# A hybrid mLSTM layer step: stabiliser rows by selector products, masks by selects, inter-chunk term scaled apart

## The chip, the cores and the metric

The kernel runs on one core of a Trainium2 chip. The metric is the device time of one execution in microseconds (us). The kernel before takes 1770.03 us, the median of three runs (1768.39 to 1771.12).

Engine names in what follows: PE is the tensor engine (PEld its weight loads), DVE the vector engine, ACT the scalar engine, POOL the GpSimd engine, SP the engine that issues most DMAs.

## What is computed

One layer of a flow-matching backbone for 128 context tokens and 256 latent tokens (384 in all, width 2048). Two parallel mixers follow one input projection: a bidirectional chunkwise mLSTM with 8 heads of 128, and a pooling mixer. Their outputs go through one output projection; a squared-ReLU MLP with hidden width 8192 follows. Scale, shift and gate of each token group come from a modulation product, `silu(c) @ ada_w`, over 6 x 2048 columns. The part that the change is about is the scan, for every head, direction and chunk of 128 tokens:

```python
b = jnp.cumsum(lfc, axis=-1)
dmat = jnp.where(mask, b[..., :, None] - b[..., None, :] + lic[..., None, :], -jnp.inf)
m_inter = b + m[..., None]
m_t = jnp.maximum(m_inter, jnp.max(dmat, axis=-1))
s = jnp.einsum('bhtd,bhsd->bhts', qc, kc) * jnp.exp(dmat - m_t[..., None])
g = jnp.exp(m_inter - m_t)
num = g[..., None] * jnp.einsum('bhtd,bhde->bhte', qc, C) + jnp.einsum('bhts,bhse->bhte', s, vc)
den = g * jnp.einsum('bhtd,bhd->bht', qc, n) + jnp.sum(s, axis=-1)
h = num / jnp.maximum(jnp.abs(den), jnp.exp(-m_t))[..., None]
```

In words: `m_t` is a stabiliser per token t; the score of tokens s and t is weighted by exp(a_s - m_t) where s lies on the right side of t (the mask), and what earlier chunks contribute (the inter-chunk term, through the state C) is weighted by g_t.

## The kernel before

Large products are made in three fp32r matmuls (high x high, high x low, low x high parts). `load_w` (L114) issues the load of a 512 KB weight block on SP, has ACT copy its high part (L126) and DVE subtract for its low part (L127); three raw blocks and four high/low blocks are in flight. `gemm_T` (L158) makes 256 columns of a product in four weight blocks, 24 matmuls of 384 columns each; a block with its matmuls is called a chunk below. Behind every chunk each `Feed` (L142) emits some steps of side work, at its own rate. In the order in time:

- Transposes of x, then u, v and the gate inputs, with the first two parts of the modulation beside them.
- `qk(0)`: q and k of heads 0 and 1, fed by `gates` (L434: cumulative sums, running maxima m, g; it ends by storing the rows m and g to `m_dram` and `g_dram`, L486 and L488), `pooling`, and modulation work.
- `qk(1)` to `qk(3)` and the o product: each `attention(hp)` (L521) handles the two heads of the pair before, in eight steps, one per chunk. Its first step loads by POOL's queue the rows m and g of the pair, broadcast to 128 partitions (`mbc`, `gbc`, L528 and L529, one buffer each), and the cached state C. Its second step does scores and transposed keys on PE; `decays` (L545) subtracts the rows from a mask of 0 and -1e30 on DVE (L548), takes the exponential on ACT (L551, 12 for a pair) and multiplies with the scores (L553). `update` (L568) makes new states. POOL multiplies q by the broadcast g (L629), so that `outputs` (L582) can accumulate the inter-chunk product in the same PSUM bank as the product with v (L589, L592). DVE, ACT and POOL then normalise (L594 to L601; the power of -0.5 is on POOL, L188), and the seventh step after transposes the heads on PE (L640).
- The modulation parts 2, 4 and 3 run beside all this: part 2 by `ada_mat` on PE (L203, feed `ada1`), parts 4 and 3 by `ada_vec` on DVE (L244, feed `ada2`): for every 512 columns 8 loads of 512 KB, each followed at once, in the same step, by its four accumulations on DVE (L255, L257). The raw blocks of both share four buffers.
- o, the output projection (w_out), then the MLP, which takes the last 1100 us.

Each engine runs its instructions in the order in which they were scheduled when the program was built; an instruction that waits holds everything behind it on its engine.

Of the kernel before, what the change touches and what calls it, by code (L numbers as in the profile page):

```python
# [13 lines left out]
P = 128  # L14
# [24 lines left out]
def hymba_kernel(  # L39
# [21 lines left out]
    # ---------------------------------------------------------------- constants and small inputs  # L61
# [26 lines left out]
    for d in range(2):  # L88
        nc.gpsimd.dma_start(mprev[32 * d:32 * d + 8, 1:2], state_m[0, 0, d, :].unsqueeze(1))
# [6 lines left out]
    # silu(c); for every contraction tile in a row of zeros, so that a window of 32 columns puts it in any pair of rows  # L96
# [9 lines left out]
    # per-channel parameters as columns: prmT [128, 80 | 96]  # L106
# [35 lines left out]
    class Feed:  # L142
        """Side work, emitted in steps between the tiles of a large product."""
# [14 lines left out]
    def gemm_T(w, cols, xs, n, evac, feeds=(), korder=(0, 1, 2, 3), name="g", hold=None):  # L158
        """Transposed products: for every 256-column group, out[128 channels, n] in two tiles; groups share the k loop."""
# [39 lines left out]
    # ---------------------------------------------------------------- adaLN  # L199
# [3 lines left out]
    def ada_mat(parts, tags=("ada",)):  # L203
        """parts: up to four (i, first channel tile), nk channel tiles each, on the tensor engine.
        Row 32 g + 2 b + (0: ctx, 1: latent) of ps holds part b's sum over the contraction tiles j = g (mod 4)."""
# [16 lines left out]
        sb = wp.tile([P, 256], F32, tag="adasb", name=f"ada_sb_{parts[0][0]}_{parts[0][1]}", bufs=2)  # L222
# [8 lines left out]
    def ada_finish(i, k0, nk, ps):  # L231
        """ps [128, nk, 2]: matrix product columns -> mod[i], with what the channel's norm weight adds to it"""
# [11 lines left out]
    def ada_vec(i, q):  # L244
        """512 channels, on the vector engine; the tensor engine adds up the partitions"""
        acc = wp.tile([P, 2, 512], F32, tag="adaacc", name=f"ada_acc_{i}_{q}", bufs=1)
        c0 = i * D + q * 512
        for t in range(8):
            raw = wp.tile([P, 2, 512], F32, tag="ada", name=f"ada_raw_{i}_{q}_{t}", bufs=N_ADA)
            nc.sync.dma_start(raw, aw[:, 2 * t:2 * t + 2, c0:c0 + 512])  # L250
            for a in range(2):
                for g in range(2):
                    cj = sg[:, g, 2 * t + a:2 * t + a + 1]
# [69 lines left out]
    # ---------------------------------------------------------------- h, and u, v, gates (token-major), k outermost  # L323
# [76 lines left out]
    # ---------------------------------------------------------------- pooling mixer  # L400
# [27 lines left out]
    m_dram = dram.tile([2, 3, 8, P], F32, name="m_dram")  # L428
    g_dram = dram.tile([2, 2, 8, P], F32, name="g_dram")
    acol = vp.tile([P, 3, 2, 8], F32, name="acol")  # L430
    ecol = vp.tile([P, 3, 8, 2], F32, name="ecol")
    nT = vp.tile([P, 16], F32, name="nT")

    def gates():  # L434
# [24 lines left out]
        aS, bS, mS, gS = [slot(n)[0:40, 0:NTOK].rearrange("p (s t) -> p s t", t=P) for n in ("aS", "bS", "mS", "gS")]  # L459
        for t in (aS, bS, mS):  # L460
            nc.gpsimd.memset(t, 0.0)
        for d in range(2):
            r = slice(32 * d, 32 * d + 8)
            nc.vector.tensor_copy(aS[r], ps_a[r, 0:NTOK].rearrange("p (s t) -> p s t", t=P))
            nc.scalar.activation(bS[r], ps_b[r, 0:NTOK].rearrange("p (s t) -> p s t", t=P), AF.Copy)
        mnew = vp.tile([40, 1], F32, name="mnew")
        for s in range(3):
            for d in range(2):
                r = slice(32 * d, 32 * d + 8)
                src = aS[r, s, :] if d == 0 else aS[r, s, ::-1]  # L470
                dst = mS[r, s, :] if d == 0 else mS[r, s, ::-1]
                nc.vector.tensor_tensor_scan(dst, src, src, mprev[r, s:s + 1], op0=ALU.max, op1=ALU.max)
                if s < 2:
                    out = mnew[r] if s == 0 else mprev[r, 2:3]
                    nc.vector.tensor_tensor(out, bS[r, s, last[d]:last[d] + 1], mS[r, s, last[d]:last[d] + 1], op=ALU.add)
                    if s == 0:
                        nc.gpsimd.dma_start(new_m[0, 0, d, :].unsqueeze(1), mnew[r])
        for s in (1, 2):
            nc.scalar.activation(gS[:, s, :], mS[:, s, :], AF.Exp, scale=-1.0, bias=mprev[:, s:s + 1])
        nc.vector.tensor_tensor(bS, bS, mS, op=ALU.add)  # L480
        nc.scalar.activation(bS, bS, AF.Exp, scale=-1.0)
        for d in range(2):
# [7 lines left out]
        for src, which in ((aS, 0), (bS, 1)):  # L490
# [557 lines left out]
```

## Time and profile before

| what | value |
|---|---|
| three timed runs | 1768.39, 1770.03, 1771.12 us |
| profiled execution: span from first to last instruction | 1766.4 us |
| its own time | not listed apart; the timed runs lie 2.0 to 4.7 us above this span |
| PE busy | 1719.2 us, 97% |
| DVE busy | 1067.4 us, 60% |
| ACT busy | 627.3 us, 36% |
| POOL busy | 129.7 us, 7% |
| granted PE clock, mean | 0.994 |
| chain that ended last | PE 86%, DMA 5%, issue 3%, DVE 2%, POOL 2%, ACT 1% |

How to read it: busy shares are means over stages with different limits. Matmuls are pipelined, so a busy PE is read from the distance between the starts of its instructions and not from the length of one. The granted clock is given in shares of full speed. Idle time of an engine is listed with what ended it.

### The profile page before, as it was taken

What the parts mean: (1) busy time and instruction counts of PE and PEld (TensorE: products, weight loads), DVE (VectorE), ACT (ScalarE), POOL (GpSimd) and SP (SyncE); (2) the same over time, 40 slices, a digit from 0 to 9 for tenths busy, and PEclk for the clock granted to TensorE, in tenths of its full rate; (3) what the DMA queues carried; (4) which work ended last, traced back from release to release, by engine and by line L of the source; (5) the groups of instructions that cost most, each with busy time, mean ns of one, the idle gap of its engine ahead of it and who ended that gap; (6) DMA issues with size and microseconds to landing.
All of it is one profiled execution on the core that took longest, in us unless ns stands there. A gap on an engine that the chain in (4) does not pass through costs nothing.

```text
span 1766.4 us, 24738 instructions
## 1 busy us (share of the span) xinstructions
PE 1719.2 (97%) x9643; PEld 1539.2 (87%) x9643; DVE 1067.4 (60%) x1756; ACT 627.3 (36%) x1047; POOL 129.7 (7%) x172
## 2 busy tenths in 40 slices
PE   6999999998999999999999999999999999999997
PEld 3777898887999989988988988988988998998986
DVE  3667877787898849763546644475444443443446
ACT  4322343443434336532432432332332332332332
POOL 0000021222101133110000000000000000000100
PEclk9999999999999999999999999999999999999999
DMA  9888988887777774574345544454434354344543
GB/s 304 279 263 286 299 261 231 253 251 213 232 238 235 237 250 156 185 225 131 120 130 162 175 130 121 130 167 122 129 120 131 120 168 131 120 130 136 165 141 107
DMA packets 250436, 326.15 MB, mean 185 GB/s; under 512 B 14096, under 2 KB 185808, under 8 KB 249936
## 3 DMA queue, kind: packets, MB, share of 16 engines
q1 hardware_dynamic: 242096, 303.74, 54.1%
q0 software_dynamic: 6560, 18.97, 4.3%
q10 hardware_dynamic: 1664, 1.87, 0.3%
q8 instruction: 75, 1.23, 0.3%
q14 instruction: 41, 0.34, 0.1%
HBM read 313.98 MB, written 10.55 MB: 184 GB/s over the span
## 4 chain that ended last, share of the span: by engine, by line
PE 86%; DMA 5%; issue 3%; DVE 2%; POOL 2%; ACT 1%; SPq 0%; ACTq 0%; DVEq 0%; POOLq 0%
PE y L855 10%; PE y L856 10%; PE y L857 10%; PE acc_w L135 9%; PE acc_w L137 9%; PE acc_w L136 9%; DMA ada_raw<-in_ada_w_dram 3%; PE acc_wo L135 3%; PE acc_wo L136 2%; PE acc_wo L137 2%; PE ada L218 2%; PE acc_o L135 1%; PE acc_o L137 1%; PE acc_o L136 1%; PE u L379 1%
## 5 line engine op out<-in xcount | busy, mean ns | idle before, releaser
L127 DVE TENSOR_TENSOR lo_w<-raw_w,hi_w 128x1024 fp32r<-128x1024 f32 x256 | 313.9, 1226 | 440.7 <-ACT hi_w L126 440.3
L126 ACT ACTIVATE hi_w<-raw_w 128x1024 fp32r<-128x1024 f32 x256 | 271.3, 1060 | 666.2 <-PE acc_w L136 302.1
L135 PE MATMUL acc_w<-h2h,hi_w 128*128 128x386 f32 x1024 | 347.8, 341 | 2.4 <-ACT h2h L805 2.4
L137 PE MATMUL acc_w<-h2h,lo_w 128*128 128x386 f32 x1024 | 347.5, 339 | 0.0
L136 PE MATMUL acc_w<-h2l,hi_w 128*128 128x386 f32 x1024 | 347.2, 339 | 0.0
L257 DVE SCALAR_TENSOR_TENSOR ada_acc<-ada_raw,sg,ada_acc 128x512 f32<-128x512 f32 x330 | 237.5, 767 | 21.8 <-DMA ada_raw<-in_ada_w_dram 21.7
L135 PEld LDWEIGHTS acc_w<-h2h,hi_w 128*128 128x128 f32 x1024 | 193.9, 190 | 5.2 <-ACT h2h L805 3.0
L136 PEld LDWEIGHTS acc_w<-h2l,hi_w 128*128 128x128 f32 x1024 | 193.8, 189 | 0.9 <-issue 0.4
L137 PEld LDWEIGHTS acc_w<-h2h,lo_w 128*128 128x128 f32 x1024 | 193.5, 189 | 0.0
L218 PE MATMUL ada<-ada_raw,cT 128*32 128x256 f32 x832 | 61.5, 397 | 5.1 <-DMA ada_raw<-in_ada_w_dram 5.0
L879 DVE TENSOR_TENSOR y<-y,y 128x512 f32<-128x512 f32 x81 | 55.7, 691 | 11.8 <-PE y L857 11.3
L126 ACT ACTIVATE hi_wo<-raw_wo 128x1024 fp32r<-128x1024 f32 x32 | 34.1, 1067 | 67.1 <-PE acc_wo L136 27.9
L846 ACT ACTIVATE z<-z,bz 128x128 f32<-128x128 f32 (+1 forms) x128 | 47.9, 442 | 11.3 <-DVE z L844 11.2
L127 DVE TENSOR_TENSOR lo_wo<-raw_wo,hi_wo 128x1024 fp32r<-128x1024 f32 x32 | 38.7, 1218 | 19.3 <-ACT hi_wo L126 19.3
L379 PE MATMUL v<-hi_v,hh 128*128 128x384 f32 (+1 forms) x144 | 49.0, 341 | 0.0
L381 PE MATMUL v<-hi_v,hl 128*128 128x384 f32 (+1 forms) x144 | 47.2, 328 | 0.0
L380 PE MATMUL v<-lo_v,hh 128*128 128x384 f32 (+1 forms) x144 | 46.9, 326 | 0.0
L774 POOL DMA_DIRECT2D gf_dram<-gfT x1 | 0.5, 519 | 626.8 <-DVE bz L843 626.8
L135 PE MATMUL acc_k<-hh,hi_k 128*128 128x384 f32 x128 | 45.4, 355 | 0.0
L218 PEld LDWEIGHTS ada<-ada_raw,cT 128*32 128x32 f32 x832 | 19.8, 110 | 28.9 <-issue 14.5
L135 PE MATMUL acc_o<-hh,hi_o 128*128 128x384 f32 x128 | 44.7, 349 | 0.0
L135 PE MATMUL acc_q<-hh,hi_q 128*128 128x384 f32 x128 | 44.4, 347 | 0.0
(940 smaller groups left out, 3621.1 us busy)
## 6 DMA issues: line engine op xcount, KB each, us to landing
raw_w<-in_w_dram SPq DMA_DIRECT2D x256, 512.0 KB, 3.7
ada_raw<-in_ada_w_dram SPq DMA_DIRECT2D x192, 512.0 KB, 5.1
raw_wo<-in_w_out_dram SPq DMA_DIRECT2D x32, 512.0 KB, 4.9
raw_u<-in_w_in_dram SPq DMA_DIRECT2D x16, 512.0 KB, 7.4
raw_q<-in_w_in_dram SPq DMA_DIRECT2D x16, 512.0 KB, 5.8
raw_k<-in_w_in_dram SPq DMA_DIRECT2D x16, 512.0 KB, 5.2
raw_o<-in_w_in_dram SPq DMA_DIRECT2D x16, 512.0 KB, 5.3
raw_v<-in_w_in_dram SPq DMA_DIRECT2D x16, 384.0 KB, 7.8
```

The costliest lines, as they stand in the source:

```text
L126: nc.scalar.activation(hi[:, 0:n], raw[:, 0:n], AF.Copy)
L127: low = lambda: nc.vector.tensor_tensor(lo[:, 0:n], raw[:, 0:n], hi[:, 0:n].bitcast(F32), op=ALU.subtract)
L135: nc.tensor.matmul(ps, lh, rh, start=start, stop=False)
L136: nc.tensor.matmul(ps, lh, rl, start=False, stop=False)
L137: mm3.ins = nc.tensor.matmul(ps, ll, rh, start=False, stop=stop).ins
L218: nc.tensor.matmul(ps[32 * g:32 * g + 32, 0:w], cT[:, j, 6 - 2 * b:38 - 2 * b], raw[:, a, :], start=b == 0 and j < 4, stop=b == n - 1 and ...
L257: nc.vector.scalar_tensor_tensor(acc[:, g, :], raw[:, a, :], cj, acc[:, g, :], op0=ALU.mult, op1=ALU.add)
L379: nc.tensor.matmul(acc[i][:, 0:n], xh[:, sl], hi[:, k, :], start=k == 0, stop=False)
L855: nc.tensor.matmul(acc, xh[:, s], hi, start=k == 8 * ch, stop=False)
L856: nc.tensor.matmul(acc, xh[:, s], lo, start=False, stop=False)
L857: nc.tensor.matmul(acc, xl[:, s], hi, start=False, stop=k == 8 * ch + 7)
L879: nc.vector.tensor_tensor(dst, acc[i], dst, op=ALU.add)
```

## The change

1. Stabiliser rows. `gates` no longer stores m and g to DRAM. It keeps m as high and low fp32r parts in one tile `mrow` of 104 partitions (high parts in partitions 0 to 39, low parts 64 higher), and a tile `pick` whose columns hold -1 in the two rows of a head. In `attention`, four matmuls per pair with a column of `pick` as broadcast weights spread -m over 128 partitions into PSUM (`mb`), in the first step.
2. Masks. The 12 exponentials of a pair read those banks, in the first step and unmasked; then two `affine_select` on POOL, one per direction, over 128 x 768 elements, put zeros outside the mask. The mask constants are gone (17 constants of 128 columns become 15). `ws4` is copied from the tile before the selects.
3. Inter-chunk term. It gets a PSUM bank of its own with q itself as weights; ACT scales it by g as a per-token column (`gcol`), DVE adds the product with v. POOL's multiplications of q are gone. The weighting of keys moves from DVE to ACT. The decay of the state is read from a column, `glast`.
4. Modulation on DVE. `ada_vec` issues each load one step ahead of the accumulations that use it; its feed has the rate 1.32 instead of 1.05 and no longer runs in `qk(0)`. Its accumulator lies in another pool; an extra PSUM bank takes its last product.

```diff
-    ada1 = Feed(mid_mat(), max(0.75, 17 * (6 - N_VEC) / 76))
-    ada2 = Feed(mid_vec(), 20 * N_VEC / 76)
+    ada1 = Feed(mid_mat(), 0.75)
+    ada2 = Feed(mid_vec(), 1.32)
...
-    qk(0, (fxt, fg_, fp_, ada1, ada2))
+    qk(0, (fxt, fg_, fp_, ada1))
...
+        raw = load(0)
+        yield
+        for t in range(16 // nj):
+            ahead = load(t + 1) if t < 16 // nj - 1 else None
...
+            raw = ahead
+            if ahead is not None:
                 yield
...
+        nc.scalar.activation(mrow, mS, AF.Copy)
         for d in range(2):
             r = slice(32 * d, 32 * d + 8)
-            for s in range(3):
-                i = tokc[d][s]
-                nc.gpsimd.dma_start(m_dram[d, i], mS[r, s, :])
-                if s:
-                    nc.gpsimd.dma_start(g_dram[d, i - 1], gS[r, s, :])
+            nc.vector.tensor_tensor(mrow[64 + 32 * d:72 + 32 * d], mS[r], mrow[r].bitcast(F32), op=ALU.subtract)
...
-        for d in range(2):
-            nc.gpsimd.dma_start(mbc[:, d], m_dram[d, :, h0:h0 + 2, :].partition_broadcast(P))
-            nc.gpsimd.dma_start(gbc[:, d], g_dram[d, :, h0:h0 + 2, :].partition_broadcast(P))
+        e = att.tile([P, 2, 2, 3, P], F32, tag="e", name=f"e_{hp}", bufs=N_E)
...
+        def decays(d, hl):
+            ps = bank(f"mb_{hp}_{d}_{hl}")
+            c = 32 * d + h0 + hl
+            nc.tensor.matmul(ps[:, 0:NTOK].rearrange("p (i t) -> p i t", t=P), pick[:, c:c + 1].to_broadcast([104, P]), mrow, start=True, stop=True)
+            for i in range(3):
+                nc.scalar.activation(e[:, d, hl, i, :], ps[:, i * P:(i + 1) * P], AF.Exp, bias=acol[:, i, d, h0 + hl:h0 + hl + 1])
...
+        for n, (i, d) in enumerate(steps):
+            nc.vector.tensor_copy(ws4[:, n], e[:, d, :, i, last[d]])
+        for d in range(2):
+            v = e[:, d].rearrange("p h i t -> p (h i) t")
+            sgn = 1 - 2 * d
+            nc.gpsimd.affine_select(v, v, [[0, 6], [sgn, P]], ALU.is_ge, 0.0, base=0, channel_multiplier=-sgn)
         yield
...
+                    for d in range(2):
                         cs = C0[d] if tokc[d][1] == i else C1[d]
-                        nc.tensor.matmul(pv[:, d, 0:129], gbc[:, d, i - 1, hl, :], cs[:, hl, :], start=False, stop=True)
+                        nc.tensor.matmul(iv[:, d], q_sb[hd][:, i * P:(i + 1) * P], cs[:, hl, :], start=True, stop=True)
+                    for d in range(2):
+                        nc.scalar.activation(num[:, d], iv[:, d], AF.Copy, scale=gcol[:, i, d, hd:hd + 1])
+                    nc.vector.tensor_tensor(num, num, intra, op=ALU.add)
```

How the order of instructions moves, at three places. First DVE, at the end of the first pair of heads: `hs_2` is the last part of that pair to be normalised, `ws_3286` and `mbc_3238` belong to the next pair. Before:

```order
L598 SCALAR_TENSOR_TENSOR hs_2_3066<-num_2_1_3079,dn_2_1_3084,hs_2_3066 128x128
L559 TENSOR_TENSOR ws_3286<-acol,mbc_3238 128x2 x2
L187 TENSOR_SCALAR rsh<-ssh 128x2
L257 SCALAR_TENSOR_TENSOR ada_acc_1_2863<-ada_raw_1_6_3250,sg,ada_acc_1_2863 128x512
L601 TENSOR_TENSOR hs_2_3066<-hs_2_3066,rsh 128x256
L257 SCALAR_TENSOR_TENSOR ada_acc_1_2863<-ada_raw_1_6_3250,sg,ada_acc_1_2863 128x512 x3
L559 TENSOR_TENSOR ws_3286<-acol,mbc_3238 128x2 x2
```

Now:

```order
L623 SCALAR_TENSOR_TENSOR hs_2_3027<-nsb_2_1_3049,dn_2_1_3055,hs_2_3027 128x128
L185 TENSOR_SCALAR rsh<-ssh 128x2
L626 TENSOR_TENSOR hs_2_3027<-hs_2_3027,rsh 128x256
L125 TENSOR_TENSOR lo_q_2_3324<-raw_q_2_3321,hi_q_2_3323 128x1024
L125 TENSOR_TENSOR lo_q_3_3375<-raw_q_3_3372,hi_q_3_3374 128x1024
L261 TENSOR_SCALAR ada_acc_512_3312<-ada_raw_512_0_3313,sg 128x512 x2
```

Neither work of the next pair nor an accumulation with a load behind it stands between the last steps of the pair any more.

Second, POOL from the loads of the first pair's state to the first power of the pair. Before:

```order
L532 DMA C_0_1_2728<-in_state_C_dram 128x2x128
L622 DMA out_dram<-C_0_0_0_2900 128x2x128
L622 DMA out_dram<-C_0_0_1_2907 128x2x128
L629 TENSOR_TENSOR gbc_2720<-q_2427,gbc_2720 128x2x128
L629 TENSOR_TENSOR gbc_2720<-q_2429,gbc_2720 128x2x128
L532 DMA C_1_0_3244<-in_state_C_dram 128x2x128
L629 TENSOR_TENSOR gbc_2720<-q_2427,gbc_2720 128x2x128
L629 TENSOR_TENSOR gbc_2720<-q_2429,gbc_2720 128x2x128
L188 TENSOR_TENSOR rsh<-rsh,mhalf 128x2
```

Now:

```order
L542 DMA C_0_1_2672<-in_state_C_dram 128x2x128
L564 AFFINE_SELECT e_2668<-e_2668 128x768 x2
L647 DMA out_dram<-C_0_0_0_2849 128x2x128
L647 DMA out_dram<-C_0_0_1_2856 128x2x128
L542 DMA C_1_0_3215<-in_state_C_dram 128x2x128
L186 TENSOR_TENSOR rsh<-rsh,mhalf 128x2
```

Two selects early in the pair take the place of four multiplications in its middle.

Third, DVE where the first pair's weights meet the scores: `e_2668` is the tile of exponentials, `lo_k_1_3000` a low part of the k product. Now:

```order
L560 COPY ws_2675<-e_2668 128x2
L125 TENSOR_TENSOR lo_k_0_2926<-raw_k_0_2923,hi_k_0_2925 128x1024
L560 COPY ws_2675<-e_2668 128x2
L125 TENSOR_TENSOR lo_k_1_3000<-raw_k_1_2997,hi_k_1_2999 128x1024
L577 TENSOR_TENSOR e_2668<-s_0_2735,e_2668 128x4x128 x2
L263 SCALAR_TENSOR_TENSOR ada_acc_0_2702<-ada_raw_0_3_2905,sg,ada_acc_0_2702 128x512 x4
```

The products with the scores (L577), which need both selects, stand in DVE's queue ahead of the following accumulations and low parts.

## Rows read from the trace of the kernel before

**Rows 1.** The page, its first line.

```profile
span 1766.4 us, 24738 instructions
```

**Rows 2.** Busy time by stretch, heads 2 to w_out: busy us of each engine, PEclk, DMA.

```profile
350.00:370.00 20.00, 17.99 (x110) 16.95 (x109) 18.17 (x49) 7.53 (x26) 9.80 (x12) 0.91 0.71 185
...
418.00:430.00 12.00, 4.05 (x26) 2.85 (x24) 3.65 (x9) 1.40 (x4) 0.70 (x1) 0.77 0.82 235
...
sum 443.00, PE 428.30 PEld 402.11 DVE 343.19 ACT 173.07 POOL 78.65; mean PE 38.94 PEld 36.56 DVE 31.20 ACT 15.73 POOL 7.15
```

**Rows 3.** Who waited for whom, 200 to 480 us: total, times, longest.

```profile
DVE ada_acc L257 <- DMA ada_raw<-in_ada_w_dram: 21.7, 11, 7.3
...
DVE ws L559 <- DMA mbc<-m_dram: 17.8, 6, 6.8
...
PE hT L640 <- DVE hs L601: 9.6, 2, 8.0
...
PE adav L270 <- ACT adav_sb L267: 3.1, 1, 3.1
...
PE ada L226 <- ACT ada_sb L223: 2.0, 1, 2.0
```

**Rows 4.** ACT in order of time, 266 to 284 us: start, length; idle before.

```profile
274.92 0.21 ACT L560 ACTIVATE ws<-ws 128x8 f32<-128x8 f32 x1 [8.87 <-DVE ws L559]
...
277.33 3.03 ACT L551 ACTIVATE mbc<-mbc,acol 128x128 f32<-128x128 f32 x10
```

**Rows 5.** DVE in order of time, 300 to 326 us.

```profile
318.24 0.23 DVE L559 TENSOR_TENSOR ws<-acol,mbc 128x2 f32<-128x2 f32 x2 [3.00 <-DMA mbc<-m_dram]
318.39 0.16 DVE L187 TENSOR_SCALAR rsh<-ssh 128x2 f32<-128x2 f32 x1
```

**Rows 6.** DVE in order of time, 405 to 432 us.

```profile
427.02 0.75 DVE L257 SCALAR_TENSOR_TENSOR ada_acc<-ada_raw,sg,ada_acc 128x512 f32<-128x512 f32 x1 [7.33 <-DMA ada_raw<-in_ada_w_dram]
```

**Rows 7.** The chain that ended last, 255 to 440 us: start, length, what.

```profile
415.85 11.14 DMA ada_raw<-in_ada_w_dram
```

**Rows 8.** DMA issues: count, size of one, median us to landing.

```profile
mbc<-m_dram POOLq DMA_DIRECT2D x8, 384.0 KB, 8.5
...
gbc<-g_dram POOLq DMA_DIRECT2D x8, 256.0 KB, 11.1
```

**Rows 9.** PE in order of time: two matmuls of k in a row.

```profile
305.03 0.34 PE L135 MATMUL acc_k<-hh,hi_k 128*128 128x384 f32 x1
305.20 0.34 PE L136 MATMUL acc_k<-hl,hi_k 128*128 128x384 f32 x1
```

**Rows 10.** PE in order of time, first pair: last keys' transposes, first heads' transposes.

```profile
278.27 0.60 PE L543 MATMUL k<-cst,k 128*128 128x128 f32 x4
...
318.30 0.38 PE L640 MATMUL hT<-cst,hs 128*128 128x128 f32 x2
```

**Rows 11.** DVE in order of time, 335 to 368 us.

```profile
344.22 2.74 DVE L257 SCALAR_TENSOR_TENSOR ada_acc<-ada_raw,sg,ada_acc 128x512 f32<-128x512 f32 x4 [1.52 <-DMA ada_raw<-in_ada_w_dram]
346.88 1.22 DVE L127 TENSOR_TENSOR lo_k<-raw_k,hi_k 128x1024 fp32r<-128x1024 f32 x1
```

**Rows 12.** Groups of instructions: count, busy us, mean ns, idle before.

```profile
L257 DVE SCALAR_TENSOR_TENSOR ada_acc<-ada_raw,sg,ada_acc 128x512 f32<-128x512 f32 x330 | 237.5, 767 | 21.8 <-DMA ada_raw<-in_ada_w_dram 21.7
...
L601 DVE TENSOR_TENSOR hs<-hs,rsh 128x256 f32<-128x256 f32 x12 | 5.1, 425 | 8.1 <-POOL rsh L188 8.1
```

**Rows 13.** Groups of instructions of POOL alone, same columns.

```profile
L823 POOL TENSOR_TENSOR sqb<-sqb,sq_x 128x384 f32<-128x384 f32 x11 | 17.4, 1578 | 20.3 <-ACT sq_x L822 19.7
L721 POOL TENSOR_TENSOR sqa<-sqa,sq_mo 128x384 f32<-128x384 f32 x13 | 16.0, 1228 | 103.8 <-ACT sq_mo L720 103.3
L629 POOL TENSOR_TENSOR gbc<-q,gbc 128x256 f32<-128x256 f32 x16 | 13.0, 829 | 6.8 <-DVE C L579 6.7
...
L188 POOL TENSOR_TENSOR rsh<-rsh,mhalf 128x2 f32<-128x2 f32 x12 | 11.2, 931 | 37.1 <-DVE rsh L187 36.9
...
L461 POOL MEMSET aS<- 40x384 f32 x1 | 0.4, 413 | 150.4 <-DVE hl L344 150.4
```

More of the change, by code (lines that the diff above doesn't have):

```diff
@@ L242, in ada_finish, with ada_vec, load @@
             nc.vector.tensor_tensor(v, v, w, op=ALU.mult)
[L244 to L251, printed above, removed]
+    def ada_vec(i, c, n, pool):
+        acc = pool.tile([P, 2, n], F32, tag="adaacc", name=f"ada_acc_{i}_{c}", bufs=1)
+        c0, nj = i * D + c, 1024 // n
+        def load(t):
+            raw = wp.tile([P, nj, n], F32, tag="ada", name=f"ada_raw_{i}_{c}_{t}", bufs=N_ADA)
+            nc.sync.dma_start(raw, aw[:, nj * t:nj * t + nj, c0:c0 + n])
+            return raw
+        raw = load(0)
+        yield
+        for t in range(16 // nj):
+            ahead = load(t + 1) if t < 16 // nj - 1 else None
+            for a in range(nj):
                 for g in range(2):
-                    cj = sg[:, g, 2 * t + a:2 * t + a + 1]
+                    cj = sg[:, g, nj * t + a:nj * t + a + 1]
                     if t == 0 and a == 0:
@@ L473, in gates @@
+                nc.vector.tensor_tensor_scan(dst, src, src, mprev[r, i:i + 1], op0=ALU.max, op1=ALU.max)
                 if s < 2:
-                    out = mnew[r] if s == 0 else mprev[r, 2:3]
-                    nc.vector.tensor_tensor(out, bS[r, s, last[d]:last[d] + 1], mS[r, s, last[d]:last[d] + 1], op=ALU.add)
+                    out = mnew[r] if s == 0 else mprev[r, tokc[d][2]:tokc[d][2] + 1]
+                    nc.vector.tensor_tensor(out, bS[r, i, last[d]:last[d] + 1], mS[r, i, last[d]:last[d] + 1], op=ALU.add)
@@ new lines, in gates @@
+        for i in (1, 2):
+            nc.scalar.activation(gS[0:40, i, :], mS[0:40, i, :], AF.Exp, scale=-1.0, bias=mprev[:, i:i + 1])
+        nc.vector.tensor_tensor(bS[0:40], bS[0:40], mS[0:40], op=ALU.add)
+        nc.scalar.activation(bS[0:40], bS[0:40], AF.Exp, scale=-1.0)
+        gd = vp.tile([40, 40], F32, name="gd")
+        for d, cols in ((0, slice(0, 32)), (1, slice(32, 40))):
+            nc.vector.tensor_scalar(gd[:, cols], ident[0:40, cols], gS[0:40, 1 + d, last[d]:last[d] + 1], None, op0=ALU.mult)
@@ L489, in gates @@
         yield
-        for src, which in ((aS, 0), (bS, 1)):
+        for src, dst in ((aS, acol), (bS, ecol), (gS, gcol)):
             ps = bank("ps_col")
-            for s in range(3):
-                nc.tensor.matmul(ps[:, s * 40:(s + 1) * 40], src[:, s, :], ident[0:40, 0:40], start=True, stop=True)
-            for s in range(3):
-                for d in range(2):
-                    i = tokc[d][s]
-                    out = acol[:, i, d, :] if which == 0 else ecol[:, i, :, d]
-                    nc.vector.tensor_copy(out, ps[:, s * 40 + 32 * d:s * 40 + 32 * d + 8])
+            i0 = 1 if dst is gcol else 0
+            for i in range(i0, 3):
+                nc.tensor.matmul(ps[:, i * 40:(i + 1) * 40], src[0:40, i, :], ident[0:40, 0:40], start=True, stop=True)
+            pv = ps[:, 0:120].rearrange("p (i r) -> p i r", r=40)
+            for d in range(2):
+                out = dst[:, :, :, d] if dst is ecol else dst[:, i0:, d, :]
+                nc.vector.tensor_copy(out, pv[:, i0:, 32 * d:32 * d + 8])
@@ L499, in gates @@
         ps = bank("ps_n0")
         nc.tensor.transpose(ps[:, 0:16], n_in, ident[0:16, 0:16])
+        nc.tensor.matmul(ps[:, 16:56], ones[0:40, :], gd, start=True, stop=True)
         nc.vector.tensor_copy(nT, ps[:, 0:16])
+        nc.vector.tensor_copy(glast, ps[:, 16:56])
         yield
@@ L523, in attention @@
         h0 = 2 * hp
-        C0, C1, pT, hss = {}, {}, {}, {}
-        mbc = att.tile([P, 2, 3, 2, P], F32, tag="mbc", name=f"mbc_{hp}", bufs=1)
-        gbc = att.tile([P, 2, 2, 2, P], F32, tag="gbc", name=f"gbc_{hp}", bufs=1)
-        for d in range(2):
-            nc.gpsimd.dma_start(mbc[:, d], m_dram[d, :, h0:h0 + 2, :].partition_broadcast(P))
-            nc.gpsimd.dma_start(gbc[:, d], g_dram[d, :, h0:h0 + 2, :].partition_broadcast(P))
+        C0, C1, hss = {}, {}, {}
+        e = att.tile([P, 2, 2, 3, P], F32, tag="e", name=f"e_{hp}", bufs=N_E)
         for d in range(2):
@@ L578, in update @@
                 for hl in range(2):
-                    nc.vector.scalar_tensor_tensor(out[:, hl, :], C0[d][:, hl, :], gbc[:, d, i - 1, hl, last[d]:last[d] + 1], pv[:, hl, :], op0=ALU.mult, op1=ALU.add)
+                    nc.vector.scalar_tensor_tensor(out[:, hl, :], C0[d][:, hl, :], glast[:, 32 * d + h0 + hl:32 * d + h0 + hl + 1], pv[:, hl, :], op0=ALU.mult, op1=ALU.add)
             return out
@@ L625, in attention @@
         C1[1] = update(2, 1, wk21)
-        for i in (1, 2):
-            for hl in range(2):
-                v = gbc[:, :, i - 1, hl, :]
-                nc.gpsimd.tensor_tensor(v, q_sb[h0 + hl][:, i * P:(i + 1) * P].unsqueeze(1).to_broadcast([P, 2, P]), v, op=ALU.mult)
         outputs(0)
@@ L768, in gate_f @@
         for q in (1, 2, 3):
-            yield from ada_vec(5, q)
+            yield from ada_vec(5, 512 * q, 512, mlp)
         ps = bank("gfT")
@@ L1006, in _consts @@
             s[32 * g + r, r] = 1.0
[L1007 removed]
+    mats = [np.eye(P, dtype=f), np.ones((P, P), f), s, le, -le, ge, -ge]
     for row in (128, 64):
```

122 lines of the change are left out of this document (58 added, 64 removed).

## The prediction

> **What bounds the kernel now.** I read the page's first line, then busy time by stretch, then the list of waits, then single engines in order of time around each wait of PE. The span is 1766.4 us [rows 1]; the three runs lie 2.0 to 4.7 us above it, their median 3.6. PE is 97% busy, so the change can win no more than PE's gaps where it acts, and it acts between the first pair of heads and w_out. There the stretches add up to 443.00 us with PE busy for 428.30 [rows 2]: 14.7 us of gaps. The list of waits names four of them, and 3.1 + 9.6 + 2.0 is the same 14.7 [rows 3].
>
> - Place 1, near 280 us, 3.1 us: PE waits for ACT's `adav_sb`, which stands in ACT's queue behind the 12 exponentials of the first pair; those run only from 277.33 on, and ACT had been idle for 8.87 us until DVE made `ws` [rows 4]. DVE in turn waits for the broadcast `mbc`, 17.8 us in six waits [rows 3].
> - Place 2, near 319 us, 1.6 us (9.6 less the longest, 8.0 [rows 3]): PE waits for `hs` to transpose the heads. DVE's queue has `ws` of the next pair ahead of `rsh`, and DVE is held 3.00 us by that pair's `mbc` [rows 5].
> - Place 3, near 362 us, 2.0 us: PE waits for ACT's `ada_sb` [rows 3]. DVE is busy for 18.17 us of the 20 here [rows 2] with accumulations whose loads had come late, and ACT's order waits with it.
> - Place 4, near 424 us, 8.0 us [rows 3], the largest: again `hs`. DVE is held 7.33 us by one `ada_raw` load [rows 6], issued at 415.85 and landed 11.14 us later [rows 7]. Just before, POOL had issued two `mbc` and two `gbc`, 384 and 256 KB each [rows 8], 1.28 MB.
>
> The gaps cost clock as well: the granted clock is 0.91 from 350 to 370 and 0.77 from 418 to 430 [rows 2]. That is 20 x 0.09 = 1.8 us, and 4.05 x 0.23 = 0.9 us on the time that PE was busy, so 2.7. In all 14.7 + 2.7 = **17.4 us** could come back.
>
> **The change part by part.**
>
> *Broadcasts gone.* 8 x 384 + 8 x 256 KB [rows 8] = 5.1 MB leave POOL's queue, and with them `mbc` as a releaser. Places 1 and 2 lose their cause: the exponentials now follow a matmul, and `ws` of the next pair no longer stands in front of `rsh`. This counts for 3.1 + 1.6.
>
> *Loads one step ahead.* An accumulation now uses a load that was issued a whole step before, and at the end of the first pair none stands between `hs_2` and the heads' transposes in DVE's queue. The load of place 4 would have had to be late by a further step. Places 3 and 4 lose their cause, 2.0 + 8.0, and the clock its 2.7. The loads that leave `qk(0)` (8 steps of 512 KB, some 4 MB) return to this stage, so its traffic stays about as it was; only its bursts go.
>
> *Matmuls added.* Four of 384 columns for a pair, 16 in all. Two such matmuls start 0.17 us apart (305.03 to 305.20) [rows 9], so 16 x 0.175 = 2.8 us, all of it on PE and so on the path; with the narrow ones that the new bank brings I take **3.2**.
>
> *Work taken from POOL and DVE.* POOL's four multiplications for a pair, 829 ns each [rows 13], and DVE's 12 mask subtractions go; the new selects, ACT's scalings and DVE's additions take their place. On ACT and POOL this is beside PE as long as DVE delivers `hs` in time, and that is the step to be costed.
>
> *DVE from the scores to `hs`.* In the first pair PE comes from the keys' transposes (278.27 + 0.60) to the heads' transposes (318.30) [rows 10]; without the 3.1 of place 1 that is 36.3 us, the cover for a pair's work. By the new order DVE has there 20 accumulations, 4 low parts and 39 short operations. Four accumulations in a row take 346.88 - 344.22 = 2.66 us, 0.665 each [rows 11]; the mean of one is 767 ns [rows 12]. A low part is 1.22 [rows 11]. The short ones lie between 0.16 for two columns [rows 5] and 0.42 for 256 [rows 12]; most are of the small kind, so I estimate 0.23 to 0.31 each. Low end: 13.3 + 4.9 + 9 = 27.2; high end: 15.3 + 4.9 + 12 = 32.2. Three powers on POOL at 0.93 [rows 13] add 3.
>
> *The select, which the trace doesn't show.* Call one A. A pair's two selects may start only behind the last copy of `ws` on DVE, and the first product with the scores follows one low part later. DVE is therefore held 2A - 1.22, plus 0.9 for the hand-over to POOL and back (as long as one of its smallest operations [rows 13]): 2A - 0.3. Bounds for A: POOL's memset writes 384 elements in 413 ns, 1.08 ns each; its slowest row reads two inputs, 1578 ns for 384, 4.1 each [rows 13]. For 768 elements A is between 0.83 and 3.16 us. A select reads one and writes one, between those kinds; I take 2.1 ns, half of the slowest: 1.6 us. A gain from it is excluded by the order, since DVE waits for it in any case. The hold is then 2.9 us: 27.2 + 3 + 2.9 = 33.1 at the low end, 38.1 at the high one, against 36.3. So between 0 and 1.8 us of stall for a pair, 0 to 7 for four; I take **3**, which is also to cover the tighter PSUM banks (the inter-chunk term takes a second one in each step) and the stores of C that the state updates wait for.
>
> What a shared port would do is bounded by two rows: the same POOL addition of 128 x 384 takes 1228 ns in one stage and 1578 in another [rows 13], so POOL is 1.3 times slower where others are busy. The Trainium skill ("SBUF — State Buffer", "Who interferes with whom") states that a DVE instruction with two SBUF inputs and a GpSimd instruction that reads SBUF exclude each other. By that rule a pair's accumulations would stand still for 2A, but also get back the 4 x 0.83 = 3.3 us of the multiplications that go: with A = 1.6 nothing changes, with A = 3.16 it is 3 us a pair more; the rows can't tell, and my sum doesn't use it.
>
> *Sum.* -17.4 + 3.2 + 3 = -11.2 us. On the profiled execution 1766.4 - 11.2 = 1755.2; plus 3.6 for the median of the runs, 1758.8, rounded **1759 us**.
>
> **The rivals.**
>
> *DVE becomes the bound of each pair.* The new order has 32 accumulations from one pair's end to the next, where 28 and 23 stood: 4 to 9 more, 2.7 to 6.9 us at 0.665 and 0.767. For it: place 3 is such a stretch, DVE 91% busy. Against it: what held DVE before was 21.7 us of waiting for loads [rows 3], and that is free now. Price: place 3 with its clock, 2.0 + 1.8 = 3.8 us, in three pairs, 11.4 instead of the residual 3: -17.4 + 3.2 + 11.4 = -2.8, so 1767.
>
> *Place 4 stays.* The change then does not do what it says of the loads: the four raw blocks are shared with the matrix part, SP issues in order, and a load one step ahead still waits for its block. For it: 11.14 us for one load [rows 7]. Against it: the burst of broadcasts beside it is gone. Then 8.0 + 0.9 stay: -17.4 + 8.9 + 3.2 + 3 = -2.3, so 1768.
>
> *The selects are dear, and it is slower.* One mechanism: products with the scores stand in DVE's order behind two selects in series, and all of DVE waits. With the low end of DVE's work the cover is used up at 2A - 0.3 = 36.3 - 30.2, A = 3.2; beyond it each us of A costs 2 a pair, 8 in all. The 14.2 us that are left of the gain (17.4 - 3.2) are lost at A = 5.0, or 6.5 ns an element. At twice the slowest row, 8.2 ns and 6.3 us, the stall is 6.1 a pair, 24.4 in all: -17.4 + 3.2 + 24.4 = +10, so 1780. For it: nothing in the trace is a compare with an index. Against it: no row of POOL is over 4.1 ns. The Trainium skill ("GPSIMD Engine Reference", section 3.1, Elementwise — side-by-side cycle accounting) puts data-dependent branching at about 12 cycles an element; by that an estimate is 768 x 12 / 1.2 GHz = 7.7 us, and the time 1791.
>
> **How the numbers follow.** Forecast 0.62, DVE as the bound 0.18, place 4 stays 0.09, dear selects 0.11. What a measurement here tells from no change is 0.2%, 3.5 us: faster means under 1766.5, slower over 1773.6. The forecast is faster; of the two rivals at 1767 and 1768, about 0.12 of their 0.27 falls below the line by the spread of their own terms, 0.15 within it. So faster 0.74, same 0.15, slower 0.11. The range: with no residual at all and only the 2.8 us of matmuls it is 1770.0 - 14.6 = 1755.4, and 2 us less if DVE's lighter work also speeds the o product; so 1753 below. Above, it takes in both nearer rivals with 2 us to spare, 1770. The dear selects and what little lies beyond are left out.
>
> **What the profile of the changed kernel would show.** From 212 to 655 us the gaps of PE should be some 3 us of stall in place of 14.7, with a clock of 1.00 in the stretches that had 0.91 and 0.77. `mbc` is no releaser any more. DVE should wait for `ada_raw` under 5 us in place of 21.7. PE should wait for `hs` at the heads' transposes under 1.5 us at once, and 16 matmuls of `mb` should stand 0.17 to 0.18 us apart. A select should last 0.8 to 3.2 us, and DVE should wait for it about twice that a pair. The prediction is wrong if a select lasts over 5 us, if PE waits for `hs` in each pair, or if a load still takes 11 us and DVE waits for it.

## The result, and the profile after

The changed kernel takes 1760.1 us (median of 4 runs, 1757.7 to 1761.5) against 1770.3 us: a ratio of 0.9946, with an interval of 0.9932 to 0.996. Forecast were 1759 us and a range of 1753 to 1770. The profiled execution has a span of 1757.1 us, 9.3 less than before [rows 1].

The view by stretch, at the places of [rows 2] and with the sum over all stretches from 212 us to the end of w_out (columns as there):

```profile
212.00:240.00 28.00, 28.00 (x188) 25.11 (x187) 13.93 (x37) 11.38 (x20) 1.06 (x2) 0.94 0.57 173
...
350.00:370.00 20.00, 20.00 (x138) 18.67 (x138) 15.49 (x43) 10.04 (x30) 1.68 (x3) 1.00 0.73 222
...
418.00:430.00 12.00, 12.00 (x84) 10.71 (x83) 9.05 (x20) 7.15 (x21) 1.81 (x2) 1.00 0.55 169
...
sum 436.00, PE 431.87 PEld 404.72 DVE 334.82 ACT 191.31 POOL 71.51; mean PE 39.26 PEld 36.79 DVE 30.44 ACT 17.39 POOL 6.50
```

PE's gaps fell from 14.7 to 436.00 - 431.87 = 4.1 us, and the clock is at 1.00 where it was 0.91 and 0.77. It is new that it is 0.94 in the stretch from 212 us.

Who waited for whom, 200 to 480 us, answering to [rows 3]:

```profile
DVE ada_acc L263 <- DMA ada_raw<-in_ada_w_dram: 15.3, 10, 4.1
...
PE inter L614 <- ACT num L624: 2.0, 2, 1.5
...
DVE e L577 <- POOL e L564: 0.8, 1, 0.8
```

The four waits of PE are gone (0.3 us of a weight load for `hs` are left), and `mbc` is no releaser. In their place PE waits 2.0 us for a PSUM bank (`inter` behind the squares that ACT writes into the bank of `num`), and in w_out, from the same list for 480 to 660 us, for `adav_sb`:

```profile
PE adaf L280 <- ACT adav_sb L276: 2.0, 1, 2.0
```

DVE still waits 15.3 us for the modulation loads.

Where the 9.3 us came from is seen from the first matmul of each large product; the trace's lists of the accumulators give it ("first to last start" behind the durations). For the changed kernel:

```profile
L133 PE MATMUL acc_q<-hh,hi_q x128: 332/337/448, 208.2 to 387.7; 128*128 128x384 f32 x128
L133 PE MATMUL acc_k<-hh,hi_k x128: 333/337/446, 242.1 to 413.7; 128*128 128x384 f32 x128
L133 PE MATMUL acc_o<-hh,hi_o x128: 333/337/448, 415.5 to 501.9; 128*128 128x384 f32 x128
```

From such starts, in us (k to o holds the first three pairs of heads):

| kernel | first q to first k | first k to o | o to w_out | w_out to MLP | median |
|---|---|---|---|---|---|
| before | 31.5 | 188.4 | 86.1 | 145.5 | 1770.3 |
| changed | 33.9 | 173.4 | 87.0 | 149.1 | 1760.1 |
| e1, no broadcasts | 31.5 | 172.8 | 85.5 | 145.4 | 1750.5 |
| e2, modulation part alone | 31.5 | 197.0 | 92.7 | 147.3 | 1782.8 |
| e3, attention part alone | 39.3 | 175.1 | 86.3 | 145.5 | 1757.0 |
| e5, the same, gates in three steps | 31.7 | 174.6 | 87.2 | 145.7 | 1752.1 |
| e6, no look-ahead | 32.3 | 175.8 | 91.5 | 150.9 | 1761.7 |
| e7, gbc alone | 31.5 | 172.9 | 85.6 | 145.4 | 1750.7 |
| e11, mbc loaded, not read | 31.5 | 179.7 | 85.5 | 145.5 | 1759.1 |
| e10, best | 31.6 | 174.7 | 86.5 | 145.6 | 1750.8 |

The change wins 15.0 us between k and o, and gives back 2.4 ahead of it, 0.9 in o and 3.6 in w_out. (The rest of the difference in span, 2.1 won before the first q and 0.9 lost in the MLP, lies in stretches that the change hardly touches. The first q starts at 206.9 to 210.5 us in the profiles of this document, also where nothing ahead of it was edited, so the 2.1 are within that spread and not a gain of the change.)

### The profile page after: what moved, and what is told of

It is laid out like the page before. It is cut to its first block, busy times and chain, and to the rows that moved or that the text cites. A ratio compares the mean times of both kernels' runs of the same rounds, so it can differ in the third digit from the quotient of the medians.

```text
span 1757.1 us, 24818 instructions
## 1 busy us (share of the span) xinstructions
PE 1721.2 (98%) x9665; PEld 1540.6 (88%) x9665; DVE 1056.9 (60%) x1744; ACT 645.5 (37%) x1108; POOL 121.7 (7%) x138
## 4 chain that ended last, share of the span: by engine, by line
PE 88%; DMA 5%; DVE 3%; issue 2%; POOL 1%; ACT 1%; SPq 0%; ACTq 0%; DVEq 0%; POOLq 0%
PE y L876 10%; PE y L877 10%; PE y L878 10%; PE acc_w L133 10%; PE acc_w L134 10%; PE acc_w L135 10%; DMA ada_raw<-in_ada_w_dram 3%; PE ada L216 2%; PE acc_wo L133 2%; PE acc_wo L135 2%; PE acc_wo L134 1%; PE acc_q L133 1%; DVE ada_acc L263 1%; PE acc_k L133 1%; PE acc_q L135 1%
```

## The experiments

Ratios are to the kernel before in the same batch, with their intervals.

### Which part gives the gain

**e1**: the kernel before without its broadcasts.

```diff
-            nc.gpsimd.dma_start(mbc[:, d], m_dram[d, :, h0:h0 + 2, :].partition_broadcast(P))
-            nc.gpsimd.dma_start(gbc[:, d], g_dram[d, :, h0:h0 + 2, :].partition_broadcast(P))
+            nc.gpsimd.memset(mbc[:, d], 0.0)
+            nc.gpsimd.memset(gbc[:, d], 1.0)
```

> The kernel before, with the eight loads of mbc and gbc replaced by memsets on POOL; it leaves the stabiliser rows and the broadcast g out of the computation. My theory: the broadcasts cause places 1 and 2 (3.1 + 1.6 us of PE waiting) and, by their burst, part of place 4 (8.0 + 0.9 us); so between 1770 - 4.7 = 1765.6 us (only the waits on mbc go) and 1770 - 13.6 = 1756.7 us (the burst alone made the load late). Rival, the late load is a matter of when it is issued: 1765 to 1766 us, with a wait of 7 to 8 us for hs still there near 424 us. Rival, the broadcasts cost nothing beside the rest: 1769 to 1771 us.

Measured: 1750.5 us, 0.9892 (0.9874 to 0.9911). This is 19.7 us less (15.8 to 22.3 by the interval), more than any theory had, and more than the whole change wins; in the profiles 16.2 us of it lie between the first k and w_out. The loads of the modulation are issued as ever, in the step that uses them, and yet the waits are nearly gone (200 to 660 us):

```profile
PE hT L640 <- DVE hs L601: 1.9, 2, 1.4
PE ada L226 <- ACT ada_sb L223: 0.4, 1, 0.4
...
DVE ada_acc L257 <- DMA ada_raw<-in_ada_w_dram: 12.2, 10, 2.6
```

So the late load of place 4 was itself an effect of the broadcasts.

**e2**: the kernel before with item 4 of the change (look-ahead, rate 1.32, not in `qk(0)`), the accumulator left in its pool.

```diff
-        for t in range(8):
+        raw = load(0)
+        yield
+        for t in range(8):
+            ahead = load(t + 1) if t < 7 else None
...
-    ada2 = Feed(mid_vec(), 20 * N_VEC / 76)
+    ada2 = Feed(mid_vec(), 1.32)
```

> The kernel before with the new modulation feed alone: each load one step ahead, rate 1.32, none of it in the first q and k. My theory: places 3 and 4 go with their clock (2.0 + 8.0 + 2.7 us), places 1 and 2 stay: 1770.3 - 12.7 = 1757.6 us. Rival, the bursts of broadcasts delay the loads all the same: places 3 and 4 stay or move, 1766 to 1772 us. Rival, DVE becomes the bound with 32 accumulations a pair: PE waits for hs in each pair, 1767 us or more.

Measured: 1782.8 us, 1.008 (1.006 to 1.01): slower by 12.5, and no theory had that (the last rival's "1767 us or more" takes in the number but not its sign: PE waits for `hs` twice, 4.2 us in all, and not in each pair). With more accumulations in each pair, place 1 comes back in several pairs, since `adav_sb` stands in ACT's queue behind the exponentials, and these behind `mbc` (200 to 480 us):

```profile
DVE ws L567 <- DMA mbc<-m_dram: 30.8, 8, 5.0
...
PE adav L278 <- ACT adav_sb L275: 15.6, 3, 5.4
```

**e3**: the changed kernel with the modulation part of before (the accumulator in its old pool, which fits with `adasb` tiles of 256 columns; so too in e5, e10 and e12).

```diff
-        raw = load(0)
-        yield
         for t in range(16 // nj):
-            ahead = load(t + 1) if t < 16 // nj - 1 else None
+            raw = load(t)
...
-    ada2 = Feed(mid_vec(), 1.32)
+    ada2 = Feed(mid_vec(), 20 * 4 / 76)
...
-    qk(0, (fxt, fg_, fp_, ada1))
+    qk(0, (fxt, fg_, fp_, ada1, ada2))
```

> The changed kernel with the modulation part as in the kernel before (load and accumulations in one step, rate 1.05, also beside the first q and k). My theory: places 1 and 2 are gone, places 3 and 4 stay if a load in the same step is what makes DVE late: 1770.3 - 4.7 + 3.2 = 1768.8 us, and as low as 1760 us if the burst of broadcasts was what made the load late. Rival, the attention part gives the whole gain: 1758 to 1761 us.

Measured: 1757.0 us, 0.9924 (0.9907 to 0.9942). The attention part gives the whole gain, and w_out is back at 145.5 us.

**e6**: the changed kernel, its loop over t as in e3 and the rate at 1.2; the feed stays out of `qk(0)`.

> The changed kernel with each modulation load issued in the step that uses it, at a rate of 1.2 (so that the accumulations keep their pace, 80 steps for 88), and still none of it beside the first q and k. The prediction's step (the look-ahead removes places 3 and 4): those 10.0 + 2.7 us return, 1770 to 1773 us. The theory after e1 to e3 (the broadcasts made the loads late, the look-ahead is worth nothing): 1757 to 1761 us, and the wait of PE for adav_sb in w_out either goes (then 1757 to 1758 us; the look-ahead caused it) or stays (then the rate did).

Measured: 1761.7 us, 0.9956 (0.9941 to 0.9972), beside 0.9946 (0.9932 to 0.996) with the look-ahead: by the medians it is worth 1.5 us, within the intervals, and not 12.7. w_out stays long without it (150.9 us, in one of the longer executions; 149.1 to 150.5 in the changed kernel, e4 and e8, which have it), so the look-ahead isn't what costs there. The sign that was to tell the two apart came out mixed: PE waits 0.5 us for `adav_sb` where it waited 2.0, but 2.4 us for `lo_wo`. What is left, by elimination and not tested apart, is the accumulations that were moved out of `qk(0)` and end later: PE has 32 products of `adav` in w_out where 24 stood before. In the changed kernel PE is busy 1.6 us longer there than before, and the wait for `adav_sb` adds 2.0.

### What of the broadcasts costs: the wait or the bytes

**e7**: e1 with `gbc` loaded as ever.

```diff
-            nc.gpsimd.dma_start(mbc[:, d], m_dram[d, :, h0:h0 + 2, :].partition_broadcast(P))
+            nc.gpsimd.memset(mbc[:, d], 0.0)
```

> The kernel before with mbc from a memset and gbc loaded as ever: 4 x 2 x 256 KB, 40 per cent of the traffic, and no DVE wait on mbc; it leaves the stabiliser rows out. e1_no_bcast, without either, took 1750.5 us. Theory, the waits on mbc in DVE's order are what costs: 1750 to 1753 us. Rival, the traffic costs, by its bytes: 1750.5 + 0.4 x 19.8 = 1758.4 us. Rival, all the waits of the late gbc show up: POOL waits for gbc, outputs come late and PE waits for hs, 1760 us or more.

Measured: 1750.7 us, 0.99 (0.9884 to 0.9915). The 2 MB of `gbc` cost nothing that these runs can tell.

**e9**: the kernel before, loads one step earlier.

```diff
             nc.gpsimd.dma_start(gbc[:, d], g_dram[d, :, h0:h0 + 2, :].partition_broadcast(P))
+        yield
...
             outputs(i)
             yield
-        yield
```

> The kernel before with the loads of mbc and gbc a step (one chunk, some 4 to 5 us) earlier than the rest of the pair, and without the empty step ahead of the heads' transposes, so that the number of steps is the same; all 5.1 MB are still loaded. Theory after e7: the waits of DVE for mbc (17.8 us) cost the 19 us, not the bytes; they go for the most part, and the heads' transposes lose one chunk of slack, 0 to 2 us a pair: 1750.6 to 1758 us. Rival, the bytes of mbc cost (60 per cent of the traffic that e7 left out): 1765 us or more, with loads of ada_raw still late by 5 us or more.

Measured: 1781.8 us, 1.0077 (1.0055 to 1.0098). The test misses its aim, for the waits were not removed: 16.0 us on `mbc` are left. DVE in order of time, 255 to 300 us:

```profile
266.59 0.23 DVE L560 TENSOR_TENSOR ws<-acol,mbc 128x2 f32<-128x2 f32 x2 [6.52 <-DMA mbc<-m_dram]
271.96 0.23 DVE L560 TENSOR_TENSOR ws<-acol,mbc 128x2 f32<-128x2 f32 x2 [5.06 <-DMA mbc<-m_dram]
```

DVE was at `ws` at 266.59 - 6.52 = 260.07, 1.5 us after the first load was issued (258.52): DVE works ahead of PE, on the low parts of later blocks, so a step is a chunk of PE's time but not of DVE's. And the empty step that was taken out had been needed: PE waits 18.4 us for `hs`, 9.6 before.

**e11**: e7, with `mbc` loaded into memory that nothing reads (one buffer of `adasb` in place of two makes room).

```diff
+        idle = (att.tile([P, 3, 2, P], F32, tag="idle", ...), dram.tile([P, 3, 2, P], F32, ...))
         for d in range(2):
-            nc.gpsimd.dma_start(mbc[:, d], m_dram[d, :, h0:h0 + 2, :].partition_broadcast(P))
+            nc.gpsimd.memset(mbc[:, d], 0.0)
+            nc.gpsimd.dma_start(idle[d], m_dram[d, :, h0:h0 + 2, :].partition_broadcast(P))
```

> The kernel before with all its broadcasts loaded, but those of mbc into memory that nothing reads (one of a pair on chip, one in DRAM), and mbc from a memset as in e1_no_bcast and e7_gbc_only; it leaves the stabiliser rows out. All 5.1 MB are moved, no instruction of DVE waits for mbc. Theory, DVE's wait in order is what costs: 1750 to 1755 us. Rival, the bytes cost: 1765 to 1770 us, with ada_raw loads that land after 9 us or more. In between: both, in that proportion.

Measured: 1759.1 us, 0.9934 (0.9916 to 0.9952), 8.4 us above e7 by the medians (6.8 in the table, between k and o). This doesn't weigh the wait against the bytes, because the bytes moved at other times than before. The four loads into DRAM (a path that the kernel before doesn't take) went out at once, long ahead of the first pair, and a modulation load behind them landed after 11.56 us (4.7 in e7); DVE stood still for it, and PE behind DVE. From POOL, the chain that ended last, DVE and PE:

```profile
234.92 2.91 POOL L530 DMA_DIRECT2D idle_dram<-m_dram  x4 [2.56 <-DMA m_dram<-mS]
241.24 11.56 DMA ada_raw<-in_ada_w_dram
252.90 0.75 DVE L257 SCALAR_TENSOR_TENSOR ada_acc<-ada_raw,sg,ada_acc 128x512 f32<-128x512 f32 x1 [7.35 <-DMA ada_raw<-in_ada_w_dram]
254.17 0.45 PE L136 MATMUL poolo<-p20l,hi_pw 128*128 128x384 f32 x1 [4.14 <-DVE p20l L182]
```

With the clock at 0.62 and 0.53 behind this gap, the 12 `poolo` products there take 5.7 us longer from first to last start than in e7, and that is most of the 6.8. The four loads on chip went out from 264.91 to 290.51, one behind the other (POOL waited 19.8 us for them), and none of these bytes moved beside the later pairs, so place 4 is not tested.

What the runs do show is where loads land late. The longest time from issue to landing of a modulation load, in 230 to 245, 262 to 300 and 300 to 450 us, is 5.7, 12.0 and 13.4 us before; 13.3, 10.4 and 7.3 in e11; 5.6, 6.2 and 8.0 in e7. It is long where the bytes of `mbc` move, also where no instruction of DVE waits for them. How the 19.7 us divide between such loads and DVE's own wait stays open.

How a wait of DVE spreads is seen in SP's queue, after 261 us. Before:

```profile
261.25 0.42 SPq L120 DMA_DIRECT2D raw_k<-in_w_in_dram  x1
267.84 0.37 SPq L214 DMA_DIRECT2D ada_raw<-in_ada_w_dram  x1
277.25 0.37 SPq L120 DMA_DIRECT2D raw_k<-in_w_in_dram  x1
```

In e1:

```profile
259.30 0.47 SPq L120 DMA_DIRECT2D raw_k<-in_w_in_dram  x1
265.57 0.37 SPq L214 DMA_DIRECT2D ada_raw<-in_ada_w_dram  x1
266.03 4.08 SPq L120 DMA_DIRECT2D raw_k<-in_w_in_dram  x2
```

DVE's hold until 274.65, where its second wait on `mbc` ends, keeps raw blocks from coming free; SP, in order, waits 9.0 us for DVE's low part and issues the next weight block at 277.25, 9.4 us after the load ahead of it (0.5 in e1). That the accumulations which pile up then make DVE late in the pairs that follow is argued from the order of events, not shown apart; and the load of place 4 itself took 11.14 us from issue to landing [rows 7], a length that e11 reaches (11.56, 13.3) with no instruction waiting for the broadcast rows.

### The narrow products of the gates

The clock of 0.94 in the first stretch comes from 228 to 236 us, where PE goes from its upper level (2.4 GHz) to the lower one (1.2 GHz, which is 0.50) and back; 0.66 is a mean of both (0.50 from 232 to 234). The changed kernel there, PE in order of time:

```profile
228.92 0.86 PE L506 MATMUL ps_col<-cst,aS 40*128 40x40 f32 x6
229.61 0.84 PE L506 MATMUL ps_col<-cst,bS 40*128 40x40 f32 x6
230.28 0.61 PE L506 MATMUL ps_col<-cst,gS 40*128 40x40 f32 x4
230.83 0.23 PE L512 MATMUL ps_n<-cst,n_in 16*128 16x16 f32 x1
230.99 0.41 PE L513 MATMUL ps_n<-gd,cst 40*128 40x40 f32 x2
231.33 2.93 PE L420 MATMUL pool<-cst,u 128*128 128x128 f32 x12
```

and its clock, by stretch:

```profile
228.00:232.00 4.00, 4.00 (x28) 3.63 (x27) 3.52 (x13) 2.23 (x5) 0.00 (x0) 0.91 0.48 133
232.00:236.00 4.00, 4.00 (x25) 3.17 (x25) 1.43 (x3) 0.98 (x2) 0.00 (x0) 0.66 0.25 76
```

Six of these 19 narrow products are new (for `gcol` and `glast`). After them the 12 `pool` products take 2.93 us.

**e4**: a step between them.

```diff
         for src, dst in ((aS, acol), (bS, ecol), (gS, gcol)):
+            if dst is gcol:
+                yield
             ps = bank("ps_col")
```

> The changed kernel with one more step in the gates: the narrow products for gcol, nT and glast come a chunk later than those for acol and ecol. Theory: the granted clock that falls to 0.66 between 228 and 236 us in the changed kernel follows on the row of 19 narrow products, 40 columns each, that PE does without a wide one between; split in 12 and 7, the clock stays at 1.00 and 1.5 to 1.8 us are won: 1758.4 us. Rival, the fall has to do with the lighter stretch (no accumulations, DMA share 0.25 to 0.5) or comes by chance: the clock falls as before, 1760 us.

Measured: 1757.8 us, 0.9933 (0.9915 to 0.9951). The clock stays at 1.00, the 12 `pool` products take 1.60 us, and first q to first k takes 32.5 us:

```profile
228.63 0.84 PE L508 MATMUL ps_col<-cst,bS 40*128 40x40 f32 x6
229.40 1.60 PE L420 MATMUL pool<-cst,u 128*128 128x128 f32 x12
```

The profile shows the 1.4 us; the runs alone, 2.3 us with overlapping intervals, don't. The fall isn't certain either: e8 has it (0.78 and 0.79), e6 with the same row of products has not (12 `pool` products in 1.60 us). So e4 alone does not show that the split kept the clock up; all four profiles with the row split (e4, e5, e10, e12) have 1.00.

**e5**: e3 with the products in three steps (`if dst is not acol: yield`).

> The attention part alone, as in e3_att_only, with the column products of the gates in three steps (acol, then ecol, then gcol with nT and glast). Theory: the stretch of the first q and k, 39.3 us in e3_att_only against 31.5 before, is long because PE waits 2.7 us for a row (bS) that DVE adds behind two accumulations, and because the clock then falls to 0.50; with the products apart both go: 1757.0 - 7.4 = 1749.6 us, and the stretch takes 32 us. Rival, the gates' chain is late whatever the steps: 1755 to 1758 us.

Measured: 1752.1 us, 0.9904 (0.9889 to 0.992). In e3 PE stood still for 2.7 us ahead of the products of `bS` (the profile names no releaser, but ACT ended `bS` 0.1 us before they start), and the clock fell to 0.50 behind that gap and the narrow products together; both are gone, and the stretch takes 31.7 us as against 39.3. This was worth 4.9 of the 7.4 us expected.

### The terms of the sum

**e8**: the changed kernel, each select four times over.

```diff
+            for _ in range(4):
-            nc.gpsimd.affine_select(v, v, ...)
+                nc.gpsimd.affine_select(v, v, ...)
```

> The changed kernel with every select done four times over (the same result), so that A is 4 x 1.29 = 5.2 us in place of 1.29. The prediction's step: cover used up at A = 3.2 us, 8 us for each us beyond it, so 1760.1 + 16 = 1776 us, with DVE waiting 2A - 0.3 = 10 us a pair for the selects. Rival, DVE comes to the products later than I took it (it waited only 0.8 us in all for the selects in the changed kernel), so that more of A is hidden: 1760 to 1766 us.

Measured: 1767.9 us, 0.9996 (0.9984 to 1.0008): 7.8 us more where my formula gave 16. DVE in order of time around the first pair's selects, which run from 276.47 to 287.12:

```profile
279.52 1.21 DVE L125 TENSOR_TENSOR lo_k<-raw_k,hi_k 128x1024 fp32r<-128x1024 f32 x1
280.66 3.88 DVE L263 SCALAR_TENSOR_TENSOR ada_acc<-ada_raw,sg,ada_acc 128x512 f32<-128x512 f32 x3
287.15 1.29 DVE L578 TENSOR_TENSOR e<-s,e 128x512 f32<-128x512 f32 x2 [2.62 <-POOL e L565]
288.36 2.73 DVE L263 SCALAR_TENSOR_TENSOR ada_acc<-ada_raw,sg,ada_acc 128x512 f32<-128x512 f32 x4
```

DVE waits 9.5 us in three pairs and not 10 in each. A select follows the two copies of its own direction only, so the first selects run while DVE still copies and makes low parts; my hold of 2A - 0.3 had both behind the last copy.

**e12**: e10 with each matmul of `mb` three times (`for _ in range(3)`).

> e10_split_square with each of the 16 matmuls that spread a stabiliser row done three times (the same result), 32 matmuls of 384 columns more. The prediction's term: 0.175 us each on the path, 1750.8 + 5.6 = 1756.4 us. Rival, PE has gaps there that take them up: 1750 to 1752 us.

Measured: 1757.2 us, 0.9927 (0.9907 to 0.9948), 6.4 us more for 32 matmuls: 0.20 us each, 3.2 us for the 16 of the change. This is rough: the intervals touch, and the stretches from the first k to w_out give 4.7 us, 0.15 each.

**e10**: e5, with the squares out of the PSUM bank.

```diff
-                nc.scalar.activation(ps[:, 260:388], hs[:, hl, :], AF.Square, ...)
+                nc.scalar.activation(num[:, 0, 0:128] if i else ps[:, 260:388], hs[:, hl, :], AF.Square, ...)
```

> e5_att_split with the squares of the normalisation (only their sum is used) written over the SBUF tile of the scaled inter-chunk term in place of the PSUM bank, which is so free earlier. Theory: PE's waits for a bank (inter behind num, 0.7 us here, 2.0 in the changed kernel) go: 1751.4 us. Rival, the bank isn't free earlier, since the sum on DVE is as late: 1752.1 us.

Measured: 1750.8 us, 0.9891 (0.9875 to 0.9907). PE's wait for a bank is gone from its list; against e5 the intervals can't tell. It computes all, and its interval lies below that of the changed kernel: the best version found, some 20 us below the kernel before and 9 below the changed one.

## Why the prediction was right, and which of its steps failed

- **Places 1 and 2, and the gaps**: right. All four waits of PE went (14.7 to 4.1 us where some 3 were forecast), and the clock with them.
- **"Loads one step ahead"**, which counted 12.7 us for places 3 and 4: this step failed. The part alone makes the kernel 12.5 us slower (e2), taking the look-ahead out costs 1.5, within the intervals (e6), and the broadcasts alone, taken away, remove those places (e1). "Broadcasts gone", put at 4.7 us, was mis-sized: it is 19.7 (e1). I read place 4 at the load that DVE stood at, and noted the burst beside it, but gave the whole wait to when the load is issued. The two errors nearly cancel, since both terms were in the forecast: 17.4 us, 19.7 measured. That the sum came out is luck in this: the same gain was put down to two causes, of which one gave all of it and the other nothing that can be told.
- **A sign that failed**: DVE was to wait under 5 us for `ada_raw`; it waits 15.3. That wait is not on PE's path, here or in e10.
- **Matmuls**: 2.8 us forecast for the 16 (3.2 with the narrow ones), 3.2 by e12's medians and 2.4 by its stretches. Four of them take 273.03 - 272.33 = 0.70 us in the changed kernel, from their start to that of the next product.
- **The select**: 1.6 us taken, 1.29 measured (median), nearly on the nearest rows. DVE's wait is 0.8 us in all, where 2.9 a pair were allowed for. The rival was thus far from deciding; e8 shows its mechanism, at half the slope. The estimate of 7.7 us from the Trainium skill ("GPSIMD Engine Reference", section 3.1) isn't borne out: a select over 768 elements takes a sixth of that.
- **The residual of 3 us** was too small, and of other content: 2.4 us ahead of the first k (six more narrow products and the clock behind them) and 3.6 in w_out, neither of which I had named. The banks, which I had, cost 2.0 us of waiting between k and o, where the changed kernel is yet only 0.6 us above e1. The sum by the runs: -19.7 + 3.2 + 2.4 + 3.6 = -10.5, measured -10.2, forecast -11.2: a larger gain and larger costs. By stretches it doesn't close as well: the 12 added matmuls between k and o should put the changed kernel some 2 us above e1 there (12 x 0.20 = 2.4), and it is 0.6 above; what wins back the rest no run shows apart.
- **DVE as the bound of each pair**, and **place 4 stays**: neither occurred; with 32 accumulations a pair, `hs` holds up one weight load of PE by 0.3 us.

## What to carry to other kernels

A wait that is long in the list may be the last link of an older one: follow it back to the first engine that stood still, and take that away alone before work is put into the last link. Broadcast loads that an in-order engine needs a step later cost far more here than the waits of PE that led back to them at once (19.7 us against 4.7): that engine stands still for them, the weight blocks behind it are issued late, and other loads that move beside them land late. When several edits come together, one of them can pay for the others: here the new feed cost 3 to 6 us (e3 beside the changed kernel, e5 beside e4) of what the attention part had won, and it shows in a stretch that it didn't aim at, w_out.

## What the runs showed of the hardware

- In e8 three accumulations on DVE took 3.88 us while selects ran on POOL (1.29 each, about the length of one select, 10.65 / 8 = 1.33), and four took 2.73 (0.68 each) after them, in the rows above. The Trainium skill ("SBUF — State Buffer", "Who interferes with whom") states that a DVE instruction with two SBUF inputs and a GpSimd instruction that reads SBUF exclude each other; this agrees. The two low parts in those rows, also with two inputs, kept 1.21 us, and there it is the select beside them that was longer (1.80 us from 279.66). With one select per direction it costs little: the mean of an accumulation is 764 ns, 767 before [rows 12].
- The granted clock can fall behind a row of narrow products between wide ones, with PE listed as busy throughout: 0.66 in the changed kernel against 1.00 in e4, and 12 `pool` products of 2.93 us against 1.60. It needn't: in e6 the same row left it at 1.00.
- 2 MB of broadcasts whose reader comes late cost nothing that can be told (e7 beside e1). 1.5 MB of them issued at once, from 234.92 to 237.83 us, made a 512 KB load that was issued at 241.24 land after 11.56 us, where the same load took 4.7 (e11 beside e7).
